# The first norm's squares from a second copy of x by rows, and an earlier first product: one streaming-encoder block on one core

## The chip, the cores and the metric

The kernel runs on one core of one Trainium2 chip. The metric is the device time of one execution in microseconds (us). Three runs of the kernel before took 929.45, 930.98 and 931.45 us; their median is 930.98 us. One more execution, taken with the profiler, took 929.6 us.

## The reference

One layer of a residual block on 512 frames of 1024 features, in float32:

```
h = x
h = h + 0.5 * swiglu(rmsnorm(h, ffn1_norm), ffn1_w_in, ffn1_w_out)       # 1024 -> 2 x 2816 -> 1024
z = rmsnorm(h, mix_norm) @ w_in                                          # one input projection
h = h + concat([conv_module(z), gated_linear_attention(z)]) @ w_out
h = h + 0.5 * swiglu(rmsnorm(h, ffn2_norm), ffn2_w_in, ffn2_w_out)
h = h + sigmoid(rmsnorm(h, ple_norm) @ ple_w_gate) * (p @ ple_w_proj)
out = rmsnorm(h, final_norm)

rmsnorm(x, g) = x * rsqrt(mean(x * x) + 1e-6) * g        # one mean for each frame
```

Only the start matters here: the first `rmsnorm` and the first products of `ffn1_w_in`. The factor of a frame's norm is the same for all of a frame's features, so the kernel multiplies x * g with the weights first and applies the factor to the results.

## The kernel before

**Layout.** x lies on the chip transposed, in eight tiles of 128 features x 512 frames (`hT`, in the rows below `h`, loaded by `load_x`). Every float32 operand is split in two parts of a shorter format (`hi` and `lo`, that is `hg` for x times its gain, `wh` and `wl` for weights), and a product is three matmuls: `wh` with x's hi, `wl` with x's hi, `wh` with x's lo. A part `hi` is a cast (ScalarE's `act.copy` or an activation with the gain as scale), and `lo` is a subtraction on VectorE.

**The start.** While the first inputs are on their way, TensorE multiplies tiles of zeros (12 matmuls in float32, each of which the trace shows as two records). Then `take(c)` runs for the eight features' chunks c = 0 to 7: 12 matmuls of 512 frames each, into four banks (`ps0`), with the weights of the first two blocks of `ffn1_w_in`, gate and up, which the host has put side by side in `first_w`. Between two takes the program makes the operands of the next: `split_w` casts a chunk of weights (for chunk 0 in two halves by VectorE, else by ScalarE) and subtracts, and `split_x` does the same for x. The gains are columns of one small tile, `col`, which ScalarE's queue loads at the start together with all other vectors of the layer.

**The norm.** ScalarE squares each x tile (`norm.add`), VectorE adds the squares up in `sqacc`, and during the last take four matmuls of that sum with a column of ones (`colsum`) give each frame's sum, 128 frames to a column. `rsqrt_mean` turns it into the factor `rs`: one step on VectorE (`ms`), a power on GpSimd, four small steps on VectorE, and between them VectorE makes the lo part of weights `a11`. The factor is needed where TensorE transposes it (`spread`, `ps<-ident,rs`), 12 matmuls after the last take; ScalarE copies the transposed factor to `bc`, and VectorE multiplies the first results with it.

**What sets the order.** On TensorE, VectorE and ScalarE each instruction is tied behind the one issued before it in the code (`in_order`), so these three run exactly in the order that is written. Loads go out on SyncE's queue (SP) in their order; a load waits for its buffer, and for the end of the load eight places before it. The tiles named `a` (`bt2`, `bt`) come from a pool of 20; raw weights from a pool of six.

**After the start** the first feed-forward runs in units (`drive`, `ffn`). Its unit for weights pair 1 is the first to use `a11` and `a12`; the transposes of the factor are queued behind that unit's first 12 matmuls. `xb.steps()` prepares sums of x (`pieces`: four activations of 256 frames; `sums1`, `sums2`: subtractions); steps 0 and 1 run right behind the takes, the others later.

Of the kernel before, what the change touches and what calls it, by code (L numbers as in the profile page):

```python
# [8 lines left out]
F32 = mybir.dt.float32  # L9
F32R = mybir.dt.float32r  # L10
I32 = mybir.dt.int32
AF = mybir.ActivationFunctionType
# [3 lines left out]
P = 128  # L16
SEQ = 512
D = 1024
DC = D // P
DFF = 2816  # L20
D_CONV = 512
WIDTH = 31
# [5 lines left out]
TB = SEQ // P  # L28
# [34 lines left out]
def block_kernel(ctx: ExitStack, tc: tile.TileContext, a: dict, out: bass.AP):  # L63
    nc = tc.nc
    pe, dve, act, pool = (Ordered(tc, e) for e in (nc.tensor, nc.vector, nc.scalar, nc.gpsimd))
# [6 lines left out]
    cp = ctx.enter_context(tc.tile_pool(name="const", bufs=1))  # L72
# [8 lines left out]
    def nm(s):  # L81
        uid[0] += 1
        return f"{s}_{uid[0]}"
# [4 lines left out]
    whole_of = {}  # L88
# [16 lines left out]
    def tmp(s, w=SEQ, dt=F32, bufs=2):  # L105
        return tp.tile([P, w], dt, tag=s, bufs=bufs, name=nm(s))
# [20 lines left out]
    def bank():  # L127
        if mode[0] == 0:
            turn_no[0] += 1
            at = turn_no[0] % 7  # L130
            if at in (3, 4):
                return fixed()
            if at in (5, 6):
                return spare()
        return psum(singles(), 3, [P, SEQ])

    def fixed():
        return psum(region("fixed"), 2, [P, SEQ])
# [4 lines left out]
    def double():  # L143
        return psum(region("fixed", "double"), 1, [P, 2, SEQ])
# [4 lines left out]
    def parted(t):  # L149
        return [t[:, 0], t[:, 1]]  # L150

    def aux():
        if mode[0] == 2:
            return fixed()
        return psum(singles(), 1, [P, SEQ], "aux")
# [11 lines left out]
    vecs = [("ffn1_norm", 8), ("mix_norm", 8), ("ffn2_norm", 8), ("ple_norm", 8),  # L167
            ("conv_b", 4), ("conv_ln_g", 4), ("conv_ln_b", 4), ("gate_b", 2), ("gla_norm", 4)]
    ncol = sum(n for _, n in vecs)
    col = cp.tile([P, ncol + 4 * WIDTH], F32, name="col")  # L170
    nc.scalar.dma_start(out=col, in_=a["columns"])
    cw = col[:, ncol:ncol + 4 * WIDTH]
    first_of, at = {}, 0
    for name, n in vecs:
        first_of[name] = at
# [1 line left out]

    def vec(name, c):
        at = first_of[name] + c
        return col[:, at:at + 1]  # L180

    warm = cp.tile([P, 1], F32, name="warm")
    act.copy(warm, ones)
    in_order(True)
    idle = bank()
    for _ in range(12):
        pe.matmul(idle[:, 0:P], zeros, zeros, start=True, stop=True)

    def split(src, s, alloc=bt):
# [14 lines left out]
    def gsplit(src, g, s):  # L204
        hi, lo = bt2(s=s)
        act.activation(hi, src, AF.Copy, scale=g)
        dve.scalar_tensor_tensor(out=lo, in0=src, scalar=g, in1=hi.bitcast(F32),
                                 op0=ALU.mult, op1=ALU.subtract)
        return hi, lo

    def raw(nk, ncol):
        return wp.tile([P, 1024], F32, tag="raw", bufs=6, name=nm("wr"))[:, :nk * ncol].rearrange(
            "p (k c) -> p k c", k=nk)
# [69 lines left out]
    def rsqrt_mean(ss, n, w, bufs=3, between=None):  # L283

        ms = tmp("ms", 16)[:, :w]
        dve.tensor_scalar(ms, ss, 1.0 / n, EPS, ALU.mult, ALU.add)
        r = tmp("rs0", 16)[:, :w]
        pool.tensor_tensor(out=r, in0=ms, in1=negh[:, :w], op=ALU.pow)
        if between is not None:
            between()  # L290
        t = tmp("rs1", 16)[:, :w]
        dve.tensor_tensor(out=t, in0=r, in1=r, op=ALU.mult)
        dve.tensor_tensor(out=t, in0=t, in1=ms, op=ALU.mult)
        dve.tensor_scalar(t, t, -0.5, 1.5, ALU.mult, ALU.add)
        rs = tmp(f"rs{bufs}", 16, bufs=bufs)[:, :w]
        dve.tensor_tensor(out=rs, in0=r, in1=t, op=ALU.mult)
        return rs

    def spread(col, copy=True):

        ps = aux()
        for j in range(TB):
            pe.transpose(ps[:, j * P:(j + 1) * P], col[:, j:j + 1].to_broadcast([P, P]), ident)
        if not copy:
            return ps
        bc = tmp("bc", bufs=1)
        act.copy(bc, ps)
        return bc

    def colsum(srcs):  # L310

        ps = aux()
        n = 0
        for s in srcs:
            for j in range(TB):
                pe.matmul(ps[:, n * TB + j:n * TB + j + 1], s[:, j * P:(j + 1) * P], ones,
                          start=True, stop=True)
            n += 1
        if n == 1:
            return ps[:, 0:TB]  # L320
        t = tmp("cs", 16)[:, :TB]
        dve.tensor_reduce(out=t, in_=ps[:, :n * TB].rearrange("p (n j) -> p j n", j=TB),
                          axis=mybir.AxisListType.X, op=ALU.add)
        return t
# [118 lines left out]
    class Left:  # L443
# [11 lines left out]
        def sum(self, out, x, y, op=ALU.subtract):  # L455
            dve.tensor_tensor(out=out, in0=x, in1=y, op=op)
# [40 lines left out]
    hT = [big.tile([P, SEQ], F32, tag="H", bufs=DC, name=nm("h")) for _ in range(DC)]  # L497
    hg = []

    def load_x(c):  # L500
        nc.sync.dma_start(out=hT[c], in_=a["xT"][c * P:(c + 1) * P])

    def split_x(c):
        hg.append(gsplit(hT[c], vec("ffn1_norm", c), "hg"))

    wraw, wpart = [raw(2, 4 * P) for _ in range(4)], []

    def load_w(k, n):
        nc.sync.dma_start(out=wraw[k // 2][:, k % 2:k % 2 + n],
                          in_=a["first_w"][k * P:(k + n) * P].rearrange("(k p) c -> p k c", p=P))  # L510

    def split_w(k, n, copy=act.copy, cols=1):
        if k % 2 == 0:
# [6 lines left out]
            copy(hi[:, :, cs], src[:, :, cs])  # L520
        dve.tensor_tensor(out=lo, in0=src, in1=hi.bitcast(F32), op=ALU.subtract)

    def take(k, between):

        wh, wl = (t[:, k % 2] for t in wpart[k // 2])
        xh, xl = hg[k]
        for i, (w, x) in enumerate(((wh, xh), (wl, xh), (wh, xl))):
            for b in (0, 2, 1, 3):
                c0 = (b // 2 + 2 * (b % 2)) * P
                pe.matmul(ps0[b], w[:, c0:c0 + P], x, start=(k == i == 0), stop=(k == DC - 1 and i == 2))  # L530
            if i == 1:
                between()

    for c in range(4):
        load_x(c)
        load_w(c, 1)
    for c in (4, 6):
# [2 lines left out]
        load_w(c, 2)  # L540
    w1 = Left(ffn1_in, 2)
    w1.fetch("a11", "a12")
    gwu = cp.tile([P, 2 * P], F32, name="gwu")
    nc.sync.dma_start(out=gwu, in_=a["gate_up"])
    ps0 = [fixed(), fixed()] + parted(double())
    split_w(0, 1, dve.tensor_copy, 2)
    split_x(0)
    norm, mid = Norm(), []
    for c in range(DC):
        take(c, lambda: mid.append(colsum([norm.acc])) if c == 7 else None)  # L550
        if c < 3:
            split_w(c + 1, 1)
        elif c in (3, 5):
            split_w(c + 1, 2)
        if c < 7:
            split_x(c + 1)
        for n in {1: (0, 1), 3: (2, 3), 4: (4,), 5: (5, 6), 6: (7,)}.get(c, ()):
            norm.add(hT[n])
        if c == 7:
            mid[0] = rsqrt_mean(mid[0], D, TB, between=lambda: w1.part("a11"))  # L560
            w1.part("a12")
    xb = Right(hg, "ffn1_norm")
    steps = xb.steps()
    steps[0]()
    steps[1]()


    made = []
# [380 lines left out]
    def sums_hooks(x, names, at):  # L949

        h = {}
        for name, key in zip(names, at):
# [14 lines left out]
    hg, norm = ffn(ffn1_in, a["ffn1_w_out"][0], xb, "mix_norm", {0: Left(ffn1_in, 0), 1: w1, 2: w2},  # L967
                   (ps0[:2], ps0[2:]), lambda: spread(mid[0]), hooks, (1,), FAR, CASTS, ADDS)
# [46 lines left out]
    def glu_value(ps):  # L1015
        a1 = tmp("u1")
        dve.tensor_tensor(out=a1, in0=ps, in1=rsb, op=ALU.mult)
        return a1
# [14 lines left out]
    mid = []  # L1033
# [14 lines left out]
    v = glu_value(pa0)  # L1048
# [226 lines left out]
    for t in range(TB):  # L1275
# [17 lines left out]
        v = bt(s="v")  # L1293
# [109 lines left out]
    w0, w1 = wf[0], wf[1]  # L1403
# [6 lines left out]
    for c in range(4):  # L1410
        dve.tensor_tensor(out=acc[c], in0=acc[c], in1=mub, op=ALU.subtract)
        sq = bt(s="lnsq")
# [31 lines left out]
    norm = Norm()  # L1444
# [68 lines left out]
    mid = []  # L1513
# [97 lines left out]
    hg, norm = ffn(ffn2_in, a["ffn2_w_out"][0], xb, "ple_norm", wf, ((g0, u0), (g1_, u1_)), mid[1], hooks, (), {("m5", 1): 4, ("m6", 2): 3, ("m1", 3): 3, ("m2", 3): 3}, {("m6", 2): 4, ("m1", 3): 4})  # L1611
# [7 lines left out]
    a11, a12, a21, a22 = of_rows(0, 0), of_rows(1, 0), of_rows(0, 1), of_rows(1, 1)  # L1619
# [225 lines left out]
    cols = [slice(0, HALF), slice(HALF, SEQ)]  # L1845
# [31 lines left out]
def layouts(v):  # L1877
    import numpy as np

    def columns(t):  # L1880
        return t.reshape(-1, P).T

    vecs = ["ffn1_norm", "mix_norm", "ffn2_norm", "ple_norm", "conv_b", "conv_ln_g", "conv_ln_b", "gate_b", "gla_norm"]
    taps = v["conv_w"][0].T.reshape(D_CONV // P, P, WIDTH).transpose(1, 0, 2).reshape(P, -1)
    w, low_rank = v["ffn1_w_in"][0], v["w_in"][0][:, -RANK:].reshape(DC, P, RANK).transpose(1, 0, 2)
    made = {name: v[name] for name in _INS}
    made["xT"] = v["x"][0].T
    made["pT"] = v["p"][0, 0].T
    made["columns"] = np.concatenate([*(columns(v[n][0]) for n in vecs), taps], axis=1)
    made["first_w"] = np.concatenate([w[:, :2 * P], w[:, DFF:DFF + 2 * P]], axis=1)  # L1890
    made["gate_up"] = np.tile(v["gate_w_up"][0], (P // RANK, 1))
    made["gate_down"] = np.concatenate([low_rank, np.zeros_like(low_rank)], axis=2)
    return {name: np.ascontiguousarray(t) for name, t in made.items()}
# [17 lines left out]
```

## Time and profile before

| | |
|---|---|
| runs | 929.45, 930.98, 931.45 us |
| the profiled execution | 929.6 us, of which 927.9 us are the span from first to last instruction |
| TensorE busy | 918.3 us (99% of the span) |
| VectorE, ScalarE, GpSimd busy | 823.0, 507.8, 58.3 us |
| chain that ended last | TensorE 99%, VectorE 1% |
| read from HBM | 93.67 MB |

How to read it: PE is TensorE, PEld its loads of the stationary operand, DVE is VectorE, ACT is ScalarE, POOL is GpSimd, SP is SyncE; a q behind the name means that engine's own instruction queue, where DMAs are issued. `out<-in` names the tiles. In brackets stands how long the engine was idle before the instruction, and who released it. Matmuls are pipelined, so the distance between two starts tells what one costs, not its duration. As nearly every instruction is recorded through one helper, all have its line, L46.

### The profile page before, as it was taken

What the parts mean: (1) busy time and instruction counts of PE and PEld (TensorE: products, weight loads), DVE (VectorE), ACT (ScalarE), POOL (GpSimd) and SP (SyncE); (2) the same over time, 40 slices, a digit from 0 to 9 for tenths busy, and PEclk for the clock granted to TensorE, in tenths of its full rate; (3) what the DMA queues carried; (4) which work ended last, traced back from release to release, by engine and by line L of the source; (5) the groups of instructions that cost most, each with busy time, mean ns of one, the idle gap of its engine ahead of it and who ended that gap; (6) DMA issues with size and microseconds to landing.
All of it is one profiled execution on the core that took longest, in us unless ns stands there. A gap on an engine that the chain in (4) does not pass through costs nothing.

```text
span 927.9 us, 12878 instructions
## 1 busy us (share of the span) xinstructions
PE 918.3 (99%) x4982; PEld 782.4 (84%) x4982; DVE 823.0 (89%) x1098; ACT 507.8 (55%) x740; POOL 58.3 (6%) x73
## 2 busy tenths in 40 slices
PE   9999999999999999999999999999999999999996
PEld 8898888888888888788877889888888888888885
DVE  6699989999999876999986789899999999997896
ACT  7664355445444574463564875355445444456883
POOL 0120000000000111001120020000000000000120
PEclk9999999999999999999999999999999999999999
DMA  9433334224322693356552563334224322348463
GB/s 325 116 91 120 108 115 128 88 80 133 118 91 65 155 260 93 74 130 138 137 137 75 153 141 109 114 114 125 87 85 130 120 91 78 110 136 244 91 113 115
DMA packets 104175, 114.44 MB, mean 123 GB/s; under 512 B 3889, under 2 KB 90289, under 8 KB 104113
## 3 DMA queue, kind: packets, MB, share of 16 engines
q1 hardware_dynamic: 97664, 94.65, 32.8%
q0 software_dynamic: 6304, 18.88, 11.2%
q8 instruction: 39, 0.64, 0.3%
q14 instruction: 24, 0.19, 0.1%
q10 hardware_dynamic: 144, 0.09, 0.0%
HBM read 93.67 MB, written 2.10 MB: 103 GB/s over the span
## 4 chain that ended last, share of the span: by engine, by line
PE 99%; DVE 1%; issue 0%; ACT 0%; POOLq 0%; DVEq 0%
PE ps L46 59%; PE pd L46 40%; DVE u L46 0%; DVE rs L46 0%; ACT yc L46 0%; DVE y L46 0%; DVE g L46 0%; DVE s L46 0%; DVE yc L46 0%; POOLq L1907 0%; DVE ms L46 0%; DVE zeros L46 0%; DVE sse L46 0%; DVEq L46 0%; POOLq L46 0%
## 5 line engine op out<-in xcount | busy, mean ns | idle before, releaser
L46 DVE TENSOR_TENSOR wl<-wr,wh 128x1024 fp32r<-128x1024 f32 (+2 forms) x161 | 188.3, 1180 | 16.3 <-ACT wh L46 16.1
L46 ACT CAST wh<-wr 128x1024 fp32r<-128x1024 f32 (+2 forms) x178 | 176.2, 1021 | 20.7 <-PE ps L46 6.4
L46 PE MATMUL pd<-hg,wh 128*128 128x512 f32 x576 | 150.0, 391 | 0.0
L46 PE MATMUL ps<-act,wh 128*128 128x512 f32 x448 | 138.3, 390 | 0.0
L46 PEld LDWEIGHTS pd<-hg,wh 128*128 128x128 f32 x576 | 105.9, 188 | 21.0 <-DVE u L46 0.4
L46 PE MATMUL ps<-hg,wh 128*128 128x512 f32 (+1 forms) x448 | 117.3, 346 | 0.0
L46 PE MATMUL pd<-t,wh 128*128 128x512 f32 x392 | 98.2, 392 | 0.0
L46 PEld LDWEIGHTS ps<-act,wh 128*128 128x128 f32 x448 | 83.1, 188 | 16.5
L46 ACT ACTIVATE s<-g 128x512 f32<-128x512 f32 x48 | 30.4, 633 | 117.9 <-DVE g L46 117.9
L46 ACT COPY sq<-pd 128x1024 f32<-128x1024 f32 x45 | 45.7, 1016 | 87.3 <-PE pd L46 52.9
L46 PEld LDWEIGHTS ps<-hg,wh 128*128 128x128 f32 x448 | 78.0, 190 | 11.3 <-issue 1.3
L46 PE MATMUL ps<-act,wl 128*128 128x512 f32 x224 | 87.1, 389 | 0.0
L46 PE MATMUL pd<-hg,wl 128*128 128x256 f32 (+1 forms) x544 | 83.9, 289 | 0.0
L46 PEld LDWEIGHTS pd<-hg,wl 128*128 128x128 f32 x544 | 75.9, 190 | 6.3
L46 PEld LDWEIGHTS pd<-t,wh 128*128 128x128 f32 x392 | 70.5, 189 | 12.6
L46 PE MATMUL ps<-hg,wl 128*128 128x512 f32 (+1 forms) x224 | 77.1, 344 | 0.0
L46 ACT CAST wh<-sm 128x1024 fp32r<-128x1024 f32 x42 | 44.0, 1051 | 54.7 <-DVE sm L46 50.5
L46 PEld LDWEIGHTS pd<-t,wl 128*128 128x128 f32 x392 | 53.5, 190 | 3.8
L46 DVE TENSOR_TENSOR wl<-sm,wh 128x1024 fp32r<-128x1024 f32 x42 | 50.9, 1219 | 4.9 <-ACT wh L46 4.9
L46 DVE TENSOR_TENSOR sq<-pd,sq 128x1024 f32<-128x1024 f32 x45 | 54.8, 1218 | 0.4 <-PE pd L46 0.4
L46 PE MATMUL ps<-wh,hg 128*128 128x512 f32 x176 | 54.8, 392 | 0.0
L46 PE MATMUL pd<-t,wl 128*128 128x256 f32 x392 | 54.7, 282 | 0.0
(307 smaller groups left out, 1636.9 us busy)
## 6 DMA issues: line engine op xcount, KB each, us to landing
wr<-in_ffn_w_in SPq DMA_DIRECT2D x84, 512.0 KB, 3.7
wr<-in_ffn_w_out SPq DMA_DIRECT2D x32, 512.0 KB, 3.5
wr<-in_w_in SPq DMA_DIRECT2D x20, 512.0 KB, 5.1
wl<-wr POOLq DMA_DIRECT2D x18, 512.0 KB, 5.3
wr<-in_ffn_w_out SPq DMA_DIRECT2D x16, 384.0 KB, 3.1
wr<-in_w_out SPq DMA_DIRECT2D x8, 512.0 KB, 4.0
wq<-in_ple_w_gate SPq DMA_DIRECT2D x8, 512.0 KB, 3.8
wl<-wq POOLq DMA_DIRECT2D x8, 512.0 KB, 4.9
```

What stands on the lines that cost most here:

```text
L46: inst = call(*args, **kwargs)
```

## The change

It touches the start, up to the norm's factor.

- The gain column of x alone (eight columns) is loaded first, as `colx`, on ScalarE's queue; the other columns follow later on SyncE's queue.
- Seven products of zeros instead of 12.
- The first chunk of `first_w` is loaded in two halves of its columns.
- The second chunk's cast goes to VectorE, in two halves, behind the split of x's second tile.
- x is loaded a second time, by rows: four tiles of 128 frames x 1024 features (`x_rows`, in rows `xr`), which take four of the pool's 20 places. ScalarE squares each with a sum over the row (`accum_out`), which gives a column of `ssx`. The squares of the transposed tiles, the sum `sqacc`, its additions and the products with ones go.
- The factor is worked out from `ssx` behind steps 0 and 1; the lo parts of `a11` and `a12` are made ahead of these.

```
-    col = cp.tile([P, ncol + 4 * WIDTH], F32, name="col")
-    nc.scalar.dma_start(out=col, in_=a["columns"])
+    col0 = cp.tile([P, DC], F32, name="colx")
+    nc.scalar.dma_start(out=col0, in_=a["columns"][:, 0:DC])
+    col = cp.tile([P, ncol + 4 * WIDTH - DC], F32, name="col")
...
-    for _ in range(12):
+    for _ in range(7):
         pe.matmul(idle[:, 0:P], zeros, zeros, start=True, stop=True)
...
+    load_x(0)
+    load_w(0, 1, slice(0, 2 * P))
+    load_w(0, 1, slice(2 * P, 4 * P))
+    for c in range(1, 4):
...
     w1.fetch("a11", "a12")
+    x_rows = []
+    for t in range(TB):
+        x_rows.append(bt2(F32, "xr")[0])
+        x_rows[t] = whole_of[id(x_rows[t])][1].rearrange("p k c -> p (k c)")
+        nc.sync.dma_start(out=x_rows[t], in_=a["x"][t * P:(t + 1) * P])
     gwu = cp.tile([P, 2 * P], F32, name="gwu")
-    nc.sync.dma_start(out=gwu, in_=a["gate_up"])
+    for to, src in ((col, a["columns"][:, DC:]), (gwu, a["gate_up"])):
+        nc.sync.dma_start(out=to, in_=src)
...
-    norm, mid = Norm(), []
     for c in range(DC):
-        take(c, lambda: mid.append(colsum([norm.acc])) if c == 7 else None)
-        if c < 3:
+        take(c)
+        if c < 7:
+            split_x(c + 1)
+        if c == 0:
+            split_w(1, 1, dve.tensor_copy, 2)
+        elif c < 3:
             split_w(c + 1, 1)
         elif c in (3, 5):
             split_w(c + 1, 2)
-        if c < 7:
-            split_x(c + 1)
-        for n in {1: (0, 1), 3: (2, 3), 4: (4,), 5: (5, 6), 6: (7,)}.get(c, ()):
-            norm.add(hT[n])
-        if c == 7:
-            mid[0] = rsqrt_mean(mid[0], D, TB, between=lambda: w1.part("a11"))
-            w1.part("a12")
     xb = Right(hg, "ffn1_norm")
     steps = xb.steps()
+    ssx = tmp("ssx", 16, bufs=1)[:, :TB]
+
+    def squared_rows(t):
+        act.activation(tmp("sq", 2 * SEQ), x_rows[t], AF.Square, accum_out=ssx[:, t:t + 1])
+
+    w1.part("a11")
+    w1.part("a12")
     steps[0]()
+    squared_rows(0)
+    squared_rows(1)
     steps[1]()
+    squared_rows(2)
+    squared_rows(3)
+    mid = [rsqrt_mean(ssx, D, TB)]
```

VectorE at the start, before (`wl_140` and `hg_144` are lo parts of chunk 0's weights and of x's first tile, `hg_162` that of the second tile):

```order
L46 CAST wh_139<-wr_112 128x256 x2
L46 TENSOR_TENSOR wl_140<-wr_112,wh_139 128x512
L46 SCALAR_TENSOR_TENSOR hg_144<-h_104,col,hg_144 128x512
L46 TENSOR_TENSOR wl_140<-wr_112,wh_139 128x512
L46 SCALAR_TENSOR_TENSOR hg_162<-h_105,col,hg_162 128x512
```

The same place in the changed kernel, on VectorE:

```order
L46 CAST wh_145<-wr_108 128x256 x2
L46 TENSOR_TENSOR wl_146<-wr_108,wh_145 128x512
L46 SCALAR_TENSOR_TENSOR hg_150<-h_100,colx,hg_150 128x512
L46 SCALAR_TENSOR_TENSOR hg_165<-h_101,colx,hg_165 128x512
L46 CAST wh_145<-wr_108 128x256 x2
L46 TENSOR_TENSOR wl_146<-wr_108,wh_145 128x512
```

The lo part of x's second tile moved ahead of the second chunk's weights, whose cast VectorE now makes too.

SyncE's queue behind the first weights, before (`wr_130` and `wr_132` are `a11` and `a12`, the next ones pair 1's other weights):

```order
L216 DMA wr_130<-in_ffn_w_in 128x4x256
L216 DMA wr_132<-in_ffn_w_in 128x4x256
L544 DMA gwu<-in_gate_up 128x256
L216 DMA wr_337<-in_ffn_w_in 128x4x256
L216 DMA wr_339<-in_ffn_w_in 128x4x256
```

And in the changed kernel:

```order
L217 DMA wr_127<-in_ffn_w_in 128x4x256
L217 DMA wr_129<-in_ffn_w_in 128x4x256
L549 DMA xr_131<-in_x 128x1024
L549 DMA xr_133<-in_x 128x1024
L549 DMA xr_135<-in_x 128x1024
L549 DMA xr_137<-in_x 128x1024
L552 DMA col<-in_columns 128x166
L552 DMA gwu<-in_gate_up 128x256
L217 DMA wr_326<-in_ffn_w_in 128x4x256
```

The four loads of x by rows stand between `a12` and the weights that follow it.

ScalarE ahead of the copy of the transposed factor (`bc`), before (`xg` are pieces of x for steps 0 and 1, `wh_341` and `wl_342` parts of pair 1's next weights):

```order
L46 ACTIVATE xg_333<-h_108,col 128x256
L46 ACTIVATE xg_333<-h_109,col 128x256
L46 CAST wh_341<-wr_337 128x1024
L46 ACTIVATE wl_342<-wr_337 128x1024
L46 COPY bc_364<-ps_359 128x512
```

And in the changed kernel:

```order
L46 ACTIVATE xg_305<-h_104,colx 128x256
L46 ACTIVATE xg_305<-h_105,colx 128x256
L46 ACTIVATE sq_311,ssx_287<-xr_135 128x1024
L46 ACTIVATE sq_313,ssx_287<-xr_137 128x1024
L46 CAST wh_330<-wr_326 128x1024
L46 ACTIVATE wl_331<-wr_326 128x1024
L46 COPY bc_353<-ps_348 128x512
```

The last two of the four squares by rows now stand behind all pieces of steps 0 and 1 (the first two stand between step 0's pieces and step 1's), and the factor can only be worked out behind them.

## Rows read from the trace of the kernel before

**Rows 1.** The page, part 4: the chain that ended last, by engine.

```profile
PE 99%; DVE 1%; issue 0%; ACT 0%; POOLq 0%; DVEq 0%
```

**Rows 2.** A wait of PE's weight loads, first 100 us: total, times, longest.

```profile
PEld ps L46 <- DVE wl L46: 0.3, 1, 0.3
```

**Rows 3.** Timeline, first 9 us: start, us, engine, instruction (second row: one narrow window).

```profile
1.12 5.04 PE L46 MATMUL ps<-zeros 128*128 128x128 f32 x24 [1.12 <-DVE zeros L46]
...
3.63 1.06 PE L46 MATMUL ps<-zeros 128*128 128x128 f32 x4
...
4.05 0.72 ACT L46 ACTIVATE hg<-h,col 128x512 fp32r<-128x512 f32 x1 [1.33 <-DMA col<-in_columns]
4.58 0.49 DVE L46 CAST wh<-wr 128x256 fp32r<-128x256 f32 x2 [3.51 <-DMA wr<-in_first_w]
5.71 0.74 DVE L46 SCALAR_TENSOR_TENSOR hg<-h,col,hg 128x512 fp32r<-128x512 f32 x1
5.92 0.48 PE L46 MATMUL ps<-hg,wh 128*128 128x512 f32 x1
6.65 0.62 ACT L46 CAST wh<-wr 128x512 fp32r<-128x512 f32 x1 [1.88 <-DMA wr<-in_first_w]
8.77 0.39 PE L46 MATMUL ps<-hg,wh 128*128 128x512 f32 x1
```

**Rows 4.** The tile of zeros: durations min/median/max (ns), first and last start.

```profile
L46 PE MATMUL ps<-zeros x24: 275/421/583, 1.1 to 5.9; 128*128 128x128 f32 x24
```

**Rows 5.** Timeline of SyncE's queue: first two x tiles, and a12.

```profile
0.80 0.39 SPq L501 DMA_DIRECT2D h<-in_xT  x1
...
1.72 0.42 SPq L501 DMA_DIRECT2D h<-in_xT  x1
...
9.33 0.37 SPq L216 DMA_DIRECT2D wr<-in_ffn_w_in  x1
```

**Rows 6.** The same three loads: KB, us from issue to landing.

```profile
h<-in_xT SPq DMA_DIRECT2D x1, 256.0 KB, 3.0
...
h<-in_xT SPq DMA_DIRECT2D x1, 256.0 KB, 3.9
...
wr<-in_ffn_w_in SPq DMA_DIRECT2D x1, 512.0 KB, 8.4
```

**Rows 7.** Busy time by stretch; the last three columns: granted clock, DMA share, GB/s.

```profile
12.00:22.00 10.00, 10.00 (x46) 8.29 (x45) 8.96 (x13) 9.09 (x14) 0.00 (x0) 1.00 1.08 357
```

**Rows 8.** Timeline, 26 to 32 us: the norm's sum and factor.

```profile
26.68 0.39 PE L46 MATMUL pd<-hg,wl 128*128 128x512 f32 x1
26.91 0.95 PE L46 MATMUL ps<-ones,sqacc 128*128 128x1 f32 x8
...
27.89 0.16 DVE L46 TENSOR_SCALAR ms<-ps 128x4 f32<-128x4 f32 x1 [5.76 <-PE ps L46]
...
29.59 0.39 PE L46 MATMUL ps<-hg,wh 128*128 128x512 f32 x1
...
30.83 0.16 DVE L46 TENSOR_TENSOR rs<-rs,rs 128x4 f32<-128x4 f32 x1
...
31.43 0.58 PEld L46 LDWEIGHTS ps<-ident,rs 128*128 128x128 f32 x4
```

**Rows 9.** Timeline of ScalarE: casts of a11 and a12, pieces of x.

```profile
20.63 1.99 ACT L46 CAST wh<-wr 128x1024 fp32r<-128x1024 f32 x2
22.52 0.90 ACT L46 ACTIVATE sqacc<-h,col 128x256 f32<-128x256 f32 x2
23.33 2.49 ACT L46 ACTIVATE xg<-h,col 128x256 f32<-128x256 f32 x6
```

**Rows 10.** Timeline of ScalarE near the end: squares with a row sum.

```profile
889.76 0.64 ACT L46 ACTIVATE u<-cv 128x512 f32<-128x512 f32 x1
890.29 0.19 ACT L46 ACTIVATION_READ_ACCUMULATOR u<-cv 128x1 f32 x1
890.39 0.62 ACT L46 ACTIVATE u<-cv 128x512 f32<-128x512 f32 x1
```

More of the change, by code (lines that the diff above doesn't have):

```diff
@@ L169, in block_kernel @@
     ncol = sum(n for _, n in vecs)
-    col = cp.tile([P, ncol + 4 * WIDTH], F32, name="col")
-    nc.scalar.dma_start(out=col, in_=a["columns"])
-    cw = col[:, ncol:ncol + 4 * WIDTH]
+    col0 = cp.tile([P, DC], F32, name="colx")
+    nc.scalar.dma_start(out=col0, in_=a["columns"][:, 0:DC])
+    col = cp.tile([P, ncol + 4 * WIDTH - DC], F32, name="col")
+    cw = col[:, ncol - DC:]
     first_of, at = {}, 0
@@ L179, in vec @@
         at = first_of[name] + c
-        return col[:, at:at + 1]
+        return col0[:, at:at + 1] if at < DC else col[:, at - DC:at - DC + 1]
     warm = cp.tile([P, 1], F32, name="warm")
@@ L506, in block_kernel, with load_w @@
     wraw, wpart = [raw(2, 4 * P) for _ in range(4)], []
-    def load_w(k, n):
-        nc.sync.dma_start(out=wraw[k // 2][:, k % 2:k % 2 + n],
-                          in_=a["first_w"][k * P:(k + n) * P].rearrange("(k p) c -> p k c", p=P))
+    def load_w(k, n, cols=slice(0, 4 * P)):
+        nc.sync.dma_start(out=wraw[k // 2][:, k % 2:k % 2 + n, cols],
+                          in_=a["first_w"][k * P:(k + n) * P, cols].rearrange("(k p) c -> p k c", p=P))
     def split_w(k, n, copy=act.copy, cols=1):
@@ L521, in split_w, with take @@
         dve.tensor_tensor(out=lo, in0=src, in1=hi.bitcast(F32), op=ALU.subtract)
-    def take(k, between):
+    def take(k):
         wh, wl = (t[:, k % 2] for t in wpart[k // 2])
@@ L530, in take @@
                 pe.matmul(ps0[b], w[:, c0:c0 + P], x, start=(k == i == 0), stop=(k == DC - 1 and i == 2))
-            if i == 1:
-                between()
-    for c in range(4):
+    load_x(0)
+    load_w(0, 1, slice(0, 2 * P))
+    load_w(0, 1, slice(2 * P, 4 * P))
+    for c in range(1, 4):
         load_x(c)
@@ L1886, in layouts @@
     made = {name: v[name] for name in _INS}
+    made["x"] = v["x"][0]
     made["xT"] = v["x"][0].T
```

## The prediction

> **What bounds the kernel now.** I read the chain that ended last first: it is TensorE for 99% [rows 1], so TensorE's own time is the kernel's, and an edit counts if it takes work or idle time from TensorE, or gives it some. Next the waits of its weight loads: behind the start there is one in the first 100 us, 0.3 us for a lo part of weights [rows 2]. So from its first real product at 5.92 us [rows 3] TensorE never pauses for long, and whatever the change gains there, it gains by letting that product start sooner or by shortening what stands up to the transposes at 31.43 us [rows 8]. Behind them the order on TensorE is the same, and VectorE and ScalarE follow the factor's copy `bc` as before; so a shift ahead of the transposes stays a shift to the end, unless something else becomes late.
>
> **The start of TensorE.** The 24 records of zeros run from 1.12 us to the first product at 5.92 [rows 3], 0.20 us each. They do not all cost the same: their durations have a median of 421 ns and a shortest of 275 [rows 4]. The profile prints no lower clock there, but the spread says that most ran at the lower of the two levels (1.2 GHz) and the last few at the higher (2.4 GHz). Four records at the lower level last 1.06 us together [rows 3], the last 0.42 of it, so they are (1.06 - 0.42) / 3 = 0.21 us apart, and at the higher level half of that. With some 0.15 us more for the first, n at the lower and 24 - n at the higher make 4.80 us for n near 20: the clock rose at about 1.12 + 0.15 + 20 x 0.21 = 5.5 us.
>
> Seven zero products are 14 records: 1.12 + 14 x 0.21 = 4.1 us, with the longer first one 4.3 at most. Then the operands decide. x's first tile lands at 0.80 + 3.0 = 3.8 us [rows 5, 6]; ScalarE took it at 4.05 because the vectors came last [rows 3]. With eight columns alone I take 3.8, and 4.05 as the worst; the hi part takes 0.72, so 4.5 to 4.8. The weights came at 4.58 [rows 3]. Half of them, 131 KB less at 357 GB/s [rows 7], is 0.37 us sooner, 4.2, and half the cast is 0.25: 4.45, at worst 4.83. First product at 4.6 us, at worst 4.9. It meets TensorE at the lower level until 5.5: there a 512-column product takes twice 0.23 us, so by 5.5 two are done, as if it had begun at full rate at 5.5 - 2 x 0.23 = 5.05. Gain: 5.92 - 5.05 = **0.87 us** (0.7 at worst, 1.1 if the clock rises with the first product).
>
> The Trainium skill ("TensorE: Matmul & The Clock Gate", Part 1) says that the throttled clock is the default and that activity releases it; that speaks against taking filler away, if the pause between the last zero product and the first real one (4.3 to 4.6) counts as lost activity. The trace of before neither shows nor excludes it; by the rule the time would be that of the second rival below.
>
> The second chunk must be ready when the first is done, at 8.77 - 0.87 = 7.9 us [rows 3]. Its x tile lands at 1.72 + 3.9 = 5.6 [rows 5, 6]; the extra load ahead may push it by one issue, to 6.1. Then hi 0.72 on ScalarE, lo 0.74 on VectorE [rows 3], which now stands ahead of the cast: 7.5 at worst; weights are there at 6.65 [rows 3]; half a cast: 7.8. It just fits; if not, TensorE waits 0.1 to 0.3 us. I take nothing. From the third chunk on TensorE comes 0.9 us sooner, ScalarE has a cast and eight squares less to do, and before there was no wait [rows 2]: nothing.
>
> **The sum's products.** From 26.68 to 29.59 us [rows 8] TensorE starts eight products and the eight records of the sum with ones: 2.91 us. Eight products alone take 8 x 0.23 = 1.84. The rest, **1.07 us**, goes: the sum's own records, the restart behind them, and the 0.3 us wait for the lo part of `a11` [rows 2], which stood on VectorE behind `ms` and so behind the sum. In the changed kernel this lo part needs only its cast, and has it long before.
>
> **The factor's new path.** It no longer hangs on TensorE but on ScalarE's queue. `a12` lands at 9.33 + 8.4 = 17.75 us [rows 5, 6]; by then ScalarE has only its cast left of the old work. A cast of 1024 columns takes 0.945 us from start to start (20.63 to 22.52 for two), a piece 0.40 (22.52 to 23.33 for two) [rows 9]. A square with a row sum costs its own time plus the read of the sum: the trace has it at 512 columns only, where the next start comes 0.63 us behind, 0.10 of it for the read (889.76, 890.29, 890.39) [rows 10]; at 1024 columns I take 0.945 + 0.10 = 1.05, and 0.945 + 0.19 = 1.14 as the upper bound, 0.945 as the lower. So: cast until 18.7, four pieces 20.3, two squares 22.4, four pieces 24.0, two squares 26.1, last read 26.25 us. From `ms` to the finished factor it took 27.89 to 30.83 + 0.16, 3.10 us [rows 8]. Factor at 26.3 + 3.1 = **29.4 us**; with the upper bound 29.8, with the lower 29.0.
>
> TensorE wants it at 31.43 - 0.87 - 1.07 = **29.49 us**. So before, the factor was 0.4 us early, and now it is 0.1 us early: what is late next is this factor, and the cover is nearly gone. By the bounds the wait is 0 to 0.5 us; I take 0.05, as the row at 1024 columns is the nearest. Two things stand behind it. VectorE waits with `ms` at its head from about 21 us; queued there are only the factor's steps and first results, which need `bc`. On ScalarE the next weights' cast and its negative (1.9 us) stand ahead of `bc`: done at 28.2 if those weights have landed by 26.
>
> **The new loads.** The four x tiles are 524 KB each; at 357 GB/s [rows 7] 1.47 us apiece, so they land at 19.2, 20.7, 22.2 and 23.6; the squares want them at 20.3, 21.4, 24.0 and 25.1: 0.7 us to spare at the tightest. The remaining columns, `gwu` and the next weights follow at about 25.7. The weights were cast at about 25.7 before [rows 9], where the pieces end, and are cast at 26.2 now; TensorE needs them about 10 us later. All weights behind them come up to 6 us later, or sooner where their buffer waited for a lo part, and none was waited for. I take nothing. The columns left out of `colx` are first needed far behind. VectorE's additions and ScalarE's squares that go lay under TensorE's work: nothing.
>
> **Sum.** 0.87 + 1.07 - 0.05 = 1.9 us off. The profiled execution, 927.9 us of span and 1.7 around it that I leave as they are, goes from 929.6 to 927.7 us; the median of the runs stands 1.4 us above it, so the time that I forecast is 930.98 - 1.9 = **929.1 us**. The three runs are 2 us apart; where a run starts later than the profiled one, TensorE wants the factor later too, and the wait is 0. Buffers of the pool of 20 get other owners all along; in the middle part that moves waits of some tenths either way, 0.5 us in the range.
>
> **The rivals.**
> - *The factor comes late* (0.14): ScalarE meets a square of 1.14 us or a late x tile, and the transposes wait 0.5 to 1.5 us. For it: ScalarE's queue is exact to 0.1 us with what TensorE wants. Against: 1.05 comes from its own rows. Net gain 0.9 on average: 930.1 us.
> - *The clock rises later* (0.10): if less filler and the pause set its rise back to as long behind the first real product as it came behind the first zero product (4.4 us), it comes at 9.0 instead of 5.5, and 3.5 us at half rate cost 1.75. Net gain 0.15: 930.8 us. Against: the pause is 0.3 us, and the real products that follow fill TensorE.
> - *Slower* (0.10): x's four tiles come late. SyncE's queue is in order and the DMA engines are full from 12 to 22 us [rows 7], at a share of 1.08; ScalarE stops at the last square, then the transposes. Each us that the last tile lands behind 25.1 is one on TensorE: from 27.1 the gain is gone, from 28.9 the kernel is slower by 1.9. The loads would have to run at 190 GB/s, half of the row's rate: about 932.9 us. Against: rows of 4 KB, longer than those of the weights that gave 357.
> - *It does as forecast* (0.66).
>
> **How the numbers follow.** A measurement of this kernel tells about 0.2% from no change, 1.9 us, and the forecast sits on that bound. The likeliest case has 1.3 to 2.6 us of gain (928.4 to 929.7) before the runs' spread, two thirds of it beyond the bound, as the start may give 1.1: 0.44 faster. Same: 0.22 + 0.14 + 0.10 = 0.46. Slower: 0.10. The range goes from 927.7 (gain 2.6 and 0.7 of spread) to 931.3 (the late clock and 0.5), and leaves out the slower case and the tails.
>
> **What would show it.** In the changed profile: first product at 4.5 to 4.9 us, at first about 0.43 us apart until the clock rises; no wait at the second chunk; no records with ones in the first 30 us; the last square's sum read at about 26.2 and the factor ready at 29.4; the transposes at 29.5 with a wait under 0.5 us; x's tiles landed by 24. Wrong would be: a wait above 0.5 us at the transposes, the slow spacing beyond 6 us, or a new wait of TensorE in the middle part.

## The result, and the profile after

The changed kernel takes 931.79 us, the median of 18 runs (930.42 to 934.01), the kernel before 930.34 us in 18 runs beside them (929.45 to 931.45): a ratio of 1.0018, 95% interval 1.0011 to 1.0024. It is 1.45 us slower; the prediction said 1.9 us faster, and the median lies 0.5 us above its range. The profiled execution took 932.57 us, 930.8 of them span, 2.9 more than before.

The chain that ended last is no longer TensorE alone [rows 1]; page of the changed kernel, part 4:

```profile
PE 91%; DMA 3%; DVE 3%; issue 2%; ACT 1%; SPq 0%; POOLq 0%; DVEq 0%; ACTq 0%
```

The waits of its weight loads in the first 100 us (total, times, longest), which answer to [rows 2]:

```profile
PEld ps L46 <- DVE wh L46: 1.3, 1, 1.3
PEld ps L46 <- DVE zeros L46: 1.1, 1, 1.1
PEld ps L46 <- DVE wl L46: 0.2, 1, 0.2
PEld ps L46 <- ACT hg L46: 0.2, 1, 0.2
```

The wait for `wh` is new. Its place is in the timeline of the first 11 us (as [rows 3]; the last two rows from a window of TensorE alone):

```profile
1.12 3.36 PE L46 MATMUL ps<-zeros 128*128 128x128 f32 x14 [1.12 <-DVE zeros L46]
...
3.60 0.72 ACT L46 ACTIVATE hg<-h,colx 128x512 fp32r<-128x512 f32 x1 [0.88 <-DMA colx<-in_columns]
3.80 0.30 DVE L46 CAST wh<-wr 128x256 fp32r<-128x256 f32 x1 [2.73 <-DMA wr<-in_first_w]
...
4.38 0.79 PE L46 MATMUL ps<-hg,wh 128*128 128x512 f32 x1
...
4.97 0.63 PE L46 MATMUL pd<-hg,wh 128*128 128x512 f32 x1
...
5.85 0.29 DVE L46 CAST wh<-wr 128x256 fp32r<-128x256 f32 x1 [1.75 <-DMA wr<-in_first_w]
...
6.20 0.79 PE L46 MATMUL ps<-hg,wh 128*128 128x512 f32 x1 [0.60 <-DVE wh L46]
...
6.56 0.72 ACT L46 ACTIVATE hg<-h,colx 128x512 fp32r<-128x512 f32 x1 [2.24 <-DMA h<-in_xT]
...
10.20 0.42 PE L46 MATMUL pd<-hg,wh 128*128 128x512 f32 x1
10.46 0.40 PE L46 MATMUL ps<-hg,wh 128*128 128x512 f32 x1
```

The first product comes at 4.38 us, sooner than forecast. Then TensorE has work for two products and waits for the other half of the weights: cast at 5.85, where the undivided load was cast at 4.58 [rows 3]. The landing times of the two halves (KB, us from issue to landing):

```profile
wr<-in_first_w SPq DMA_DIRECT2D x1, 128.0 KB, 2.5
...
wr<-in_first_w SPq DMA_DIRECT2D x1, 128.0 KB, 4.1
```

Up to 10.20 the products are 0.43 us apart, behind it 0.23: TensorE ran at the lower level (1.2 GHz) until then, 4.7 us longer than before. The second chunk starts at 10.46, 1.69 us later than before [rows 3].

Up to the transposes (ScalarE's last sum, VectorE's two ends of the factor, and the transposes, as [rows 8]):

```profile
26.79 0.18 ACT L46 ACTIVATION_READ_ACCUMULATOR sq<-xr 128x1 f32 x1
...
27.01 0.17 DVE L46 TENSOR_SCALAR ms<-ssx 128x4 f32<-128x4 f32 x1 [5.07 <-ACT sq L46]
...
28.99 0.16 DVE L46 TENSOR_TENSOR rs<-rs,rs 128x4 f32<-128x4 f32 x1
...
32.04 0.58 PEld L46 LDWEIGHTS ps<-ident,rs 128*128 128x128 f32 x4
```

The factor is ready at 29.15, the transposes start at 32.04, 0.61 us later than before [rows 8]: of the 1.69 us lost, 1.08 came back. This stays so for 300 us. The rest is lost far from anything the diff touches. At 347 us the kernel before has no wait (first fence: its ScalarE); in the changed one weights of `w_in` come 3.1 us late to ScalarE, and TensorE follows (second fence: its ScalarE and TensorE):

```profile
339.54 1.05 ACT L46 CAST wh<-wr 128x1024 fp32r<-128x1024 f32 x1 [1.30 <-PE pd L46]
```

```profile
342.64 1.05 ACT L46 CAST wh<-wr 128x1024 fp32r<-128x1024 f32 x1 [3.12 <-DMA wr<-in_w_in]
...
349.41 3.94 PEld L46 LDWEIGHTS ps<-hg,wa 128*128 128x128 f32 x18 [1.31 <-issue]
349.44 4.78 PE L46 MATMUL ps<-hg,wa 128*128 128x512 f32 x19 [0.92 <-DVE h L46]
```

The late load's own row, and that of the load in its place in the kernel before (KB, us from issue to landing):

```profile
wr<-in_w_in SPq DMA_DIRECT2D x1, 512.0 KB, 12.9
```

```profile
wr<-in_w_in SPq DMA_DIRECT2D x1, 512.0 KB, 10.7
```

Behind ScalarE's late cast stand its activations `hg<-h`, behind these VectorE, and TensorE waits at the end of that queue. Between 340 and 360 us the changed kernel falls back by 2.15 us, and by another 0.55 at 889 us, where TensorE waits 0.7 us for one of GpSimd's accumulating transfers (loads that add to what the tile holds):

```profile
PEld ps L46 <- DMA wl<-wq: 0.7, 1, 0.7
```

0.61 + 2.15 + 0.55 = 3.3 us of TensorE's time in this execution.

### The profile page after: what moved, and what is told of

It is laid out like the page before. It is cut to its first block, busy times and chain, and to the rows that moved or that the text cites. A ratio compares the mean times of both kernels' runs of the same rounds, so it can differ in the third digit from the quotient of the medians.

```text
span 930.8 us, 12842 instructions
## 1 busy us (share of the span) xinstructions
PE 919.5 (99%) x4964; PEld 780.9 (84%) x4964; DVE 818.8 (88%) x1093; ACT 507.4 (55%) x739; POOL 57.6 (6%) x73
## 4 chain that ended last, share of the span: by engine, by line
PE 91%; DMA 3%; DVE 3%; issue 2%; ACT 1%; SPq 0%; POOLq 0%; DVEq 0%; ACTq 0%
PE ps L46 54%; PE pd L46 37%; DMA wr<-in_w_in 2%; DVE wl L46 1%; DMA wl<-wq 1%; DMA wr<-in_first_w 0%; DVE hg L46 0%; ACT wh L46 0%; DVE sqacc L46 0%; DVE sq L46 0%; DVE g L46 0%; ACT hg L46 0%; ACT act L46 0%; ACT wa L46 0%; DVE u L46 0%
## 5 line engine op out<-in xcount | busy, mean ns | idle before, releaser
L46 PEld LDWEIGHTS ps<-hg,wh 128*128 128x128 f32 x448 | 78.5, 191 | 12.9 <-DVE wh L46 1.3
L46 DVE SCALAR_TENSOR_TENSOR cv<-glu,col,cv 128x502 f32<-128x502 f32 (+24 forms) x90 | 61.8, 728 | 0.3
```

Of the source, the lines that this page charges most:

```text
L46: inst = call(*args, **kwargs)
```

## The experiments

All times in one table. "Up at" is where products (or zeros) come closer, 0.43 to 0.23 us, so where TensorE reached the higher level (2.4 GHz). "Records" counts TensorE's matmul records, and "packet" is the time of a transfer; the second group below explains both. Starts and waits are of the one profiled execution of each. A ratio compares with runs of the kernel before taken beside that version (their medians lie between 930.15 and 930.77 us), so medians of different groups compare to about 0.6 us.

| version | median us | ratio to before (95%) | up at | 2nd chunk | transposes | records | packet | wait at 347 |
|---|---|---|---|---|---|---|---|---|
| before | 930.34 | | 5.5 | 8.77 | 31.43 | 4982 | 322.5 | 0 |
| changed | 931.79 | 1.0018 (1.0011 to 1.0024) | 10.2 | 10.46 | 32.04 | 4964 | 331.7 | 1.3 |
| changed, 2nd profile | 932.02 (one) | | 5.7 | 8.98 | 30.52 | 4964 | 330.0 | 1.7 |
| changed, 3rd profile | 932.22 (one) | | 4.2 | 9.04 | 30.68 | 4964 | 329.7 | 1.7 |
| e1: 12 zeros | 929.24 | 0.9988 (0.9979 to 0.9997) | 6.4 | 9.16 | 30.70 | 4974 | 324.1 | 0 |
| e2: whole load | 931.13 | 1.0010 (1.0001 to 1.0019) | 5.0 | 8.96 | 30.61 | 4964 | 330.0 | 1.9 |
| e3: before, 7 zeros | 930.00 | 0.9999 (0.9990 to 1.0008) | 4.1 | 8.50 | 31.32 | 4972 | 324.6 | 0 |
| e4: 12 zeros, whole load | 928.57 | 0.9984 (0.9975 to 0.9992) | 7.0 | 9.45 | 30.98 | 4974 | 324.4 | 0 |
| x1: changed + 5 tiny | 929.74 | 0.9990 (0.9982 to 0.9999) | 4.3 | 8.78 | 30.42 | 4974 | 324.0 | 0 |
| x2: e4, 7 long zeros | 932.06 | 1.0018 (1.0009 to 1.0026) | 5.4 | 8.88 | 30.52 | 4964 | 330.1 | 1.4 |
| x3: e2 + 5 tiny | 930.23 | 0.9993 (0.9983 to 1.0002) | 10.0 | 10.18 | 31.73 | 4974 | 325.0 | 0 |
| x5: changed + 5 tiny at 30 us | 930.09 | 0.9999 (0.9991 to 1.0008) | 5.1 | 8.59 | 30.87 | 4974 | 324.2 | 0 |
| e5: before + rows' sum | 929.12 | 0.9984 (0.9976 to 0.9993) | 6.9 | 9.39 | 30.93 | 4974 | 324.4 | 0 |
| b4: whole load, 10 zeros | 929.00 | 0.9985 (0.9976 to 0.9994) | 5.7 | 8.76 | 30.29 | 4974 | 323.8 | 0 |
| b6: b4, x tile 1 by ScalarE | 929.56 | 0.9990 (0.9982 to 0.9999) | 4.4 | 8.89 | 30.43 | 4974 | 323.9 | 0 |
| z3: whole load, 3 zeros | 931.31 | 1.0010 (1.0001 to 1.0019) | 8.9 | 9.51 | 32.01 | 4974 | 325.2 | 0 |

**The start, part by part.** The first theory (A) was that seven zero products and the pause hold the clock down; its rival (B), that only the late half costs.

e1 has the first of these edits to the changed kernel, e2 the second, e4 both:

```diff
-    for _ in range(7):
+    for _ in range(12):
         pe.matmul(idle[:, 0:P], zeros, zeros, start=True, stop=True)
```

```diff
-    load_w(0, 1, slice(0, 2 * P))
-    load_w(0, 1, slice(2 * P, 4 * P))
+    load_w(0, 1)
```

e3 is the kernel before with `range(7)` in place of `range(12)` there. What was expected, in the order e1 to e4 (10.69 in e1's text, 10.7 for short, is the second chunk's second product; its first starts at 10.46):

> The changed kernel with twelve zero products in place of seven; the halved first load stays. Theory A (the seven products and the pause behind the second real product hold TensorE at the lower of its two clock levels until 10 us): the zeros run to about 5.9 us, the clock rises at 5.5 as in the kernel before, the second half of the weights is cast by 6.2, so products start near 6.2, 0.23 us apart, and the second chunk starts at 9.0 (10.69 in the changed kernel): 1.7 us off the changed kernel, 930.1. Theory B (only the late second half of the first weights costs, the clock does not matter): the second chunk stays at 10.7 and the time at 931.8.

> The changed kernel with the first chunk's weights in one load; seven zero products stay. Theory B: the cast comes at 4.6 or before, no pause in the first chunk, the clock rises at 5.5, second chunk at 7.9 us, 2.8 us off the changed kernel, 929.0. Theory A: products from 4.6 us are 0.43 us apart, and the clock rises late all the same, at 9 to 10 us, so the second chunk comes at 9.6: 1.1 us off at most, 930.7.

> The kernel before with seven zero products and nothing else changed. My forecast's step: the first product moves from 5.92 to about 4.9 us, the clock rises at 5.5 as before, 0.6 us off, 929.7. Theory A: the products are 0.43 us apart until 9 us or later, the second chunk comes at 9.3 to 10.0 in place of 8.77, 0.5 to 1.2 us on top, 930.8 to 931.5.

> The changed kernel with twelve zero products and the first chunk's weights in one load, so that of the start only x's column alone and the second chunk's cast by VectorE are left. Theory A: first product 5.9, second chunk at 8.8 as before, the transposes 1.1 to 1.3 us sooner than in the kernel before; if the wait at 348 us does not come, 929.2, about 2.6 off the changed kernel; if it is a fixed part of the change, 931.3. A theory by which the rows' sum itself costs time (its four loads) would give no less than 930.3.

Neither theory holds. Without the pause and with seven zeros (e2) the clock is up at 5.0 us, the first chunk is done by 7.5, and TensorE then waits for the second chunk, whose x tile reached ScalarE only at 7.11. e2's TensorE, two ends of the first chunk and the second chunk:

```profile
4.68 0.63 PE L46 MATMUL ps<-hg,wh 128*128 128x512 f32 x1 [0.21 <-DVE wh L46]
...
7.47 0.39 PE L46 MATMUL pd<-hg,wh 128*128 128x512 f32 x1
8.96 0.47 PE L46 MATMUL ps<-hg,wh 128*128 128x512 f32 x1 [1.11 <-DVE wh L46]
```

e3 too gains 0.27 us at the second chunk, and 0.11 at the transposes, where I had 0.6 at the end. And e1 came out 0.9 us better than A allowed: its start gave back 1.3 us, but the wait at 347 us had gone as well. Of the changed kernel's versions, those with twelve zeros lacked that wait; e2, with seven, had it, though its transposes came within 0.1 us of e1's. e3 has seven zeros too and no wait, but it keeps the sum's products with ones. That made the next group.

**The length of the program.** On the page's part 3 queue q8 (kind: instruction) moves 39 packets, 0.64 MB, so 16 KB each: by its count TensorE's own program, as one comes for 128 of its 4982 matmul records on average. One of them falls at 322 to 325 us in the kernel before, in e1, e3 and e4, and at 330 to 332 us in the changed kernel and in e2. The rows of q8 (packets, MB, share) for 320 to 327 us of the kernel before, and for 327 to 335 us of the changed one:

```profile
q8 instruction: 1, 0.02, 0.8%
```

```profile
q8 instruction: 1, 0.02, 0.9%
```

The DMA engines are full in both stretches, but with other transfers. The changed kernel by stretch (last three columns: granted clock, DMA share, GB/s):

```profile
320.00:327.00 7.00, 7.00 (x32) 5.81 (x31) 4.30 (x6) 5.03 (x9) 1.87 (x3) 1.00 1.00 166
327.00:335.00 8.00, 8.00 (x37) 6.60 (x37) 2.94 (x4) 7.20 (x13) 3.45 (x4) 1.00 1.14 298
```

The first, at 166 GB/s, is nearly all GpSimd's accumulating transfers; in the second, at 298, the loads of `w_in` run that ScalarE casts at 340. So theory C: fewer instructions ahead of it moved this packet in among those loads. The table's records tell how many fewer: the changed kernel has 18 less than the kernel before, ten of zeros and eight of the sum with ones. The eight alone (e1, e4) or the ten alone (e3) leave the packet at 324 to 325 us. Its rival D: chance, or the start's timing. x1 (from the changed kernel) and x3 (from e2) add these lines behind the zeros, x5 has them in the first `spread`, ahead of its transposes:

```diff
+    for _ in range(5):
+        pe.matmul(idle[0:32, 0:1], zeros[:, 0:32], zeros[:, 0:1], start=True, stop=True)
```

x2 is e4 with as many columns of zeros in fewer products:

```diff
-    for _ in range(12):
-        pe.matmul(idle[:, 0:P], zeros, zeros, start=True, stop=True)
+    for _ in range(7):
+        pe.matmul(idle[:, 0:220], zeros[:, 0:P], zeros, start=True, stop=True)
```

Expected of x1, x2, x3, a second profile of the changed kernel, and x5:

> The changed kernel with five more zero products behind the seven, of 32 columns of weights and one column of data each: TensorE's program is as long as with twelve zero products, at next to no time. Theory C (the wait at 348 us comes from where the load of TensorE's program falls: a packet of 16 KB on the instruction queue, at 331.7 us in the changed kernel and 330.0 with the whole first load, at 322.5 to 324.6 us in the four profiles without the wait, and the w_in loads keep the DMA engines full between): the packet comes at 324 to 326 us, the wait at 348 goes, and with it the wait at 889 us, about 2 us off the changed kernel, 929.8. Theory D (the wait comes from the seven zero products' earlier or later start of the loads, or by chance of each execution): the time stays at 931.8. The start has its two products and its pause again: by theory A the clock rises at about 10 us again; if it rises at 5 to 7, the late rise of the one profile was chance.

> The version with twelve zero products and the whole first load (928.57 us), with seven zero products of 220 columns in place of twelve of 128: the same columns of zeros, the same start, ten instructions of TensorE and ten weight loads fewer. Theory C: the program's packet falls at 330 to 332 us again, the wait at 348 us is back, 1.5 to 2.5 us slower, 930.3 to 931.0. Theory D: the start is that of the version with twelve, so the time is too, 928.6.

> The changed kernel with the whole first load (931.13 us) and the same five tiny products behind its seven. Theory C: packet at 324 to 326 us, no wait at 348 us, 1.5 to 2.5 us faster, 928.6 to 929.6. Theory D: 931.1.

> The changed kernel once more, one look. Theory C: the program's packet at 331 to 332 us again, a wait of 1 to 2 us of TensorE at 347 to 349 us again. Theory D as chance of each execution: the wait is there in some looks only. Theory A: the clock rises at 9 to 10.5 us again, with the pause behind the second product; as chance: at 5 to 7 us.

> The changed kernel with its seven zero products and the five tiny ones moved from the start to just ahead of the transposes of the first factor, at 30 us. Theory C (what decides at 348 us is only how many instructions of TensorE stand before it): packet at 324 to 325 us, no wait at 348 us, 929.9. Theory D' (the five tiny products helped because they fill the gap ahead of the first product): the packet's place has no part, 931.8.

C holds in both directions. Five tiny products take 2.05 us off the changed kernel (x1), and the same five put at 30 us, behind the start, 1.7 (x5: its ten records there are 0.03 us apart, and with the pauses around them the first transposing product comes some 0.5 us later behind the second chunk than in the versions without them). Five products fewer, for the same columns of zeros, put 3.5 us on e4 (x2), though its second chunk starts sooner. x5, with the wait gone (ScalarE has its weights at 337.84), then the changed kernel's second profile and x2 (ScalarE each):

```profile
337.84 1.04 ACT L46 CAST wh<-wr 128x1024 fp32r<-128x1024 f32 x1
342.63 1.05 ACT L46 CAST wh<-wr 128x1024 fp32r<-128x1024 f32 x1 [0.61 <-DMA wr<-in_w_in]
```

```profile
341.55 1.05 ACT L46 CAST wh<-wr 128x1024 fp32r<-128x1024 f32 x1 [3.51 <-DMA wr<-in_w_in]
```

```profile
341.25 1.05 ACT L46 CAST wh<-wr 128x1024 fp32r<-128x1024 f32 x1 [3.32 <-DMA wr<-in_w_in]
```

All five profiles with 4964 records have the wait (1.3 to 1.9 us), none of the eleven others. Between 340 and 360 us the five lose 2.15 to 2.8 us against the kernel before, the ten other versions 0.3 to 1.0: the length costs about 1.9 us. That the number of instructions decides, and that it takes both the zeros and the sum's products, is shown. How the packet delays the load is inferred: it takes 1.15 to 1.2 us there, a load seems to be spread over all 16 engines and so to end with the last (the trace has 16 end packets of 4 bytes for each of SyncE's 200 loads), and the trace shows a few of the load's 512-byte packets left over until 341 us among GpSimd's 2048-byte ones. The late load takes 12.9 to 13.6 us to land in the five, 7.0 to 7.4 in ten others. But in the kernel before it took 10.7, with no packet of q8 behind its issue and two of 8 KB from another instruction queue (q14; e3 has two as well, and 7.3); there it landed at 339.4, and TensorE did not wait. So the 16 KB packet is not the only thing that goes with a late landing.

x3 missed its number, 930.23 instead of 928.6 to 929.6, for another reason: its runs lie in two groups, four at 927.9 to 928.8 and eight at 929.7 to 931.4, and its profile, 930.9, has the late clock, with no pause in the first chunk. The changed kernel's second profile has the pause, but the clock up at 5.7. So A's pause is not what makes it late. TensorE in x3, first chunk's end:

```profile
9.04 0.63 PE L46 MATMUL pd<-hg,wh 128*128 128x512 f32 x1
9.46 0.63 PE L46 MATMUL ps<-hg,wh 128*128 128x512 f32 x1
9.89 0.46 PE L46 MATMUL pd<-hg,wh 128*128 128x512 f32 x1
10.18 0.40 PE L46 MATMUL ps<-hg,wh 128*128 128x512 f32 x1
10.42 0.39 PE L46 MATMUL pd<-hg,wh 128*128 128x512 f32 x1
```

**The rows' sum alone, and how many zeros.**

e5 is e4 with one tile of all columns again, as in the kernel before, and the old order between the takes:

```diff
         take(c)
-        if c < 7:
-            split_x(c + 1)
-        if c == 0:
-            split_w(1, 1, dve.tensor_copy, 2)
-        elif c < 3:
+        if c < 3:
             split_w(c + 1, 1)
         elif c in (3, 5):
             split_w(c + 1, 2)
+        if c < 7:
+            split_x(c + 1)
```

b4 is e2 with `range(10)` zeros and two tiny products behind them, z3 is e2 with `range(3)` and nine tiny ones at 30 us. b6 is b4 with the second x tile on ScalarE's queue, right behind the column:

```diff
     nc.scalar.dma_start(out=col0, in_=a["columns"][:, 0:DC])
+    nc.scalar.dma_start(out=hT[1], in_=a["xT"][P:2 * P])
...
-        load_x(c)
+        if c > 1:
+            load_x(c)
```

Expected of e5, b4, b6, z3, and a third profile of the changed kernel:

> The kernel before with nothing but the norm's sum by rows of x (and the four loads that it needs, the remaining columns in one load as before, twelve zero products, ScalarE's cast of the second chunk's weights). Theory: the sum's products on TensorE and the wait behind them were worth 0.9 to 1.3 us (start of the second chunk to the transposes, in eight profiles), and nothing else in the kernel costs, with the program's packet at 324 to 325 us: 929.2, 1.1 off the kernel before. If x's column alone and the cast by VectorE, which the version at 928.57 has too, are worth something, it is above 928.6 by that much. Rival (the rows' loads cost as much as the products): 930.3.

> The changed kernel with the whole first load, ten zero products and two tiny ones, so that zeros end at about 5.4 us instead of 4.2 and 5.9, with the program as long as with twelve. Theory E (the first product's time is worth nothing before the second chunk is ready at 8.2 to 9.0 us, and fewer zeros only let the clock rise late in some executions): second chunk at 8.6 to 9.1 us, 928.6, as with twelve. Theory F (each zero product less is 0.4 us off, if the clock rises in time): 927.9.

> The same with the second x tile's load issued from ScalarE's queue, right behind the column's, at 1.2 us instead of 1.7. Theory E: the second chunk is what the start waits for; if its x tile lands 0.5 us or more sooner, the second chunk starts at 8.0 to 8.4 us, and the time is 928.0 to 928.3. If the tile lands as late as in the other kernels (DMA engines, not the issue, set it), 928.6.

> The changed kernel with the whole first load, three zero products (done at 2.4 us, so TensorE stands still until the first product at 4.7), and nine tiny ones ahead of the transposes at 30 us that keep the program as long as with twelve. Theory G (fewer zeros let the clock rise later): the rise comes at 8 to 11 us in this profile, the second chunk at 9.7 to 10.3 us, the median at 929.8 to 930.4, and no run is at the 928 us of the fast ones with seven. Theory H (a late rise is chance, whatever the zeros): rise at 4 to 7 us, second chunk at 8.6 to 9.1, median 928.6 to 929.2.

> The changed kernel, one more look. By the program's length: packet at 330 to 332 us, a wait of 1 to 2 us at 346 to 349 us, as in its two other profiles. Clock: rise at 4 to 7 us or at about 10 us, either has been seen.

e5 came out at its number: the sum by rows alone is worth 1.26 us. e4 is 0.55 below it and b4 0.12; the intervals are 0.8 us wide to either side, so what x's column alone and the cast by VectorE are worth is not told. b4 came out near E's 928.6, and F's 927.9 lies below its interval: its zeros end 0.4 us before e4's, and it is no faster. The reason that E gave is not shown by it, as neither e4 nor b4 waits for the second chunk, which starts 0.23 us behind the last product of the first in both. b6 missed: the second x tile came sooner, but SyncE's queue now took the weights first and the first x tile second, which reached ScalarE at 5.26 us in place of 3.7, with the second right behind:

```profile
5.26 1.33 ACT L46 ACTIVATE hg<-h,colx 128x512 fp32r<-128x512 f32 x2 [2.06 <-DMA h<-in_xT]
```

The first product waited for it until 6.04, and the second chunk began at 8.89. So whether an earlier second tile would help stays open. z3 fits G: with three zeros the clock was up at 8.9, and none of its runs came below 930.37. The second chunk came a little sooner than G had it, at 9.51, and the median is 0.9 us above the upper end of what I had; the nine tiny products, which put the transposes back by about 0.7, account for most of that. The changed kernel's third profile has the packet at 329.7, the wait of 1.7 us, and the clock up at 4.2.

## Why the prediction was wrong

**The steps that failed** are two: the start's 0.87 us, which came out as a loss, and the nothing (0.5 us in the range) that I had for the middle part, where 1.9 us were lost, the larger share. Two of the three signs that the prediction had named for being wrong came in the first profile: the slow spacing beyond 6 us and a new wait of TensorE in the middle part.

**The start's 0.87 us.** What failed in it is the sentence "It just fits; if not, TensorE waits 0.1 to 0.3 us. I take nothing." The second chunk was to start at 7.9 us. In the three profiles of the changed kernel it starts at 8.98, 9.04 and 10.46; before it was 8.77. So the term is a loss of 0.2 to 0.3 us, or 1.7 with the late clock. Three things were mis-sized in it:
- *The second half.* I priced "half of them" by its bytes (0.37 us sooner). The first half was sooner, cast at 3.80; the second came 1.27 us after the time of the whole load. A load that waits in line behind another has its own time to landing.
- *The second x tile.* I had it landed by 6.1 us at the latest. ScalarE took it at 6.56, 6.93 and 7.18 in the three profiles, in e2, with one load less ahead of it, at 7.11, and in x3, with the same loads as e2, at 5.52. Nothing in one profile of the kernel before showed how far landings vary in the first 8 us.
- *The clock.* I took its rise as fixed at 5.5 us. It came at 4.1 to 10.2 us. With seven zeros it was late (10.0, 10.2) in two of eight profiles, with ten or more (or x2's seven long ones) in none of seven, with three in the only one. This is the second rival ("the clock rises later", 9.0, 0.10), right in kind, and near in its cost: with the late rise the second chunk comes 1.4 to 1.5 us later than in the changed kernel's two other profiles, and in x3 1.2 later than in e2, where the rival had 1.75. But it is a chance of each execution, not a new fixed time. Two of eight against none of seven is too few to prove that the number of zeros decides. The spread of the runs does not prove it either: it is 2.2 to 3.6 us in the versions with seven zeros and 1.3 to 1.9 in the other versions, but the kernel before, with twelve, spreads by 2.0 to 3.3 in its groups of 15 to 33 runs.

The Trainium skill ("TensorE: Matmul & The Clock Gate", Part 1) says that how many products run at the lower level differs from run to run of one kernel. The rows agree: 10.2, 5.7 and 4.2 us in three profiles of the same kernel.

**The sum's products: right.** From the second chunk's start to the transposes it was 22.66 us before, and 21.54 to 21.64 in all twelve profiles of kernels that sum by rows and have nothing added there: 1.02 to 1.12 us less, forecast 1.07. e5 alone is 1.26 us faster.

**The factor's path: right, with more room than thought.** ScalarE's squares start 1.04 us apart (21.12, 22.16; forecast 1.05), and from the first step to the finished factor it is 2.15 us, not 3.10, as no lo part stands between the steps any more. The factor was ready at 29.15 to 29.6 us in the changed kernel, 1.1 us or more ahead of the transposes; it was never waited for. The rivals of the late factor and of x's late tiles fell.

**What no term or rival had:** the wait at 347 us, about 1.9 us. I gave the middle part 0.5 us in the range for other owners of buffers. Its cause is the 18 records of TensorE fewer (with their weight loads), ten of zeros and eight of the sum: together they move the load of TensorE's program, and neither does alone (e3; e1, e4 and e5). The page of the profile had the row (q8, 39 packets, its time given as a share of the same 16 DMA engines), and I did not ask where they lie. The Trainium skill ("Runtime: NRT & Kernel Launch", Instruction fetch mechanics) says that the program comes in blocks of 16 KiB and that crossing into one is mostly hidden. The size agrees with the trace (16,384 bytes); hidden it must be in most of the 39 places, as TensorE is busy for 99% of the changed kernel's span too, but at 347 us TensorE lost time.

**The sum of the median:** 1.05 off for the sum, 0.2 to 0.5 on for the start (the late clock in a part of the executions), 1.9 on for the program's packet. That gives 1.05 to 1.35 of the measured 1.45. The wait at 889 us, which all three profiles have (0.55 to 1.15 us), would bring more than the rest, but four versions without the wait at 347 have it too; how often it comes in the runs of either kernel is not known.

**Better than both:** e4 (928.57), b4 (929.00) and e5 (929.12) keep the rows' sum with ten or twelve zeros and 4974 records; each interval lies below 1.

## What to carry to other kernels

Before pricing an earlier first product, look for what the second and the next chunk need: the start is worth no more than the operand that comes next allows, and landings in the first microseconds can vary by more than the gain (5.52 and 7.11 us for one tile in x3 and e2, whose loads are the same). Do not drop warm-up products because the first real operand comes sooner: with seven the clock rose late in two of eight profiles, with ten or more in none of seven. When a change alters the number of instructions, compare where the program's own packets (the instruction queues on the page) fall against loads that are waited for; here five cheap products moved one back.

## What the runs showed of the hardware that was not expected

- A 16 KB packet of TensorE's program took 0.88 to 1.66 us in most places of the kernel before and after, and up to 2.6 in one. In the versions where one moved by some 7 us, in among loads that were wanted soon, TensorE lost about 1.9 us 15 us later.
- The wait at 889 us goes with the time that the packet just ahead of GpSimd's accumulating transfers took: in the nine profiles where it took 1.15 us or more TensorE waited there and fell back 0.35 to 1.15 us, in the seven with 1.12 or less it did not. Whether the packet is slow because of those transfers or they because of it, no run here separates.
- A product of zeros with 32 columns of weights and one of data takes 0.03 us for each of its two records at the higher level (x5, z3), and a row of them ahead of the transposes cost some 0.2 us more: the cheapest filler seen here for moving a program.
